# Order of the first loads, the first root and two steps of transposes in the head of an encoder layer

## The chip, the cores and the metric

The kernel runs on one core of a Trainium2 chip. The metric is the device time of one execution in microseconds (us), as the median of several runs; beside it stands one execution that the hardware profiler recorded. TensorE multiplies, VectorE (DVE) and ScalarE (ACT) work on tiles, GpSimd (POOL) and SyncE (SP) mostly start transfers. A transfer that SP starts goes through SP's queue, one that ScalarE starts through ScalarE's own.

## What is computed

One layer on x of 1024 tokens by 1024 features, all float32: half a SwiGLU step, two groups of attention heads on a common projection, and another half SwiGLU step, each between two RMS norms. The change touches only the start of the first step:

```python
def rmsnorm(x, g):
    xf = x.astype(jnp.float32)
    y = xf * lax.rsqrt(jnp.mean(xf * xf, axis=-1, keepdims=True) + NORM_EPS)
    return (y * g.astype(jnp.float32)).astype(x.dtype)

def swiglu(x, w_gate, w_up, w_down):
    return (jax.nn.silu(x @ w_gate) * (x @ w_up)) @ w_down

    ...
        h = swiglu(rmsnorm(x, ffn1_pre_g[l]), ffn1_w_gate[l], ffn1_w_up[l], ffn1_w_down[l])
        x = x + 0.5 * rmsnorm(h, ffn1_post_g[l])
```

## The kernel before

**Tiles.** x is cut into eight tiles of 128 tokens by 1024 features; the head of the kernel works on tiles 0 to 3. A tile is normalised (square and sum, root, scale by the row's root and the gain), and then turned by TensorE's transposes (L174), 128 x 128 at a time, four for a half of 512 features, because the products contract over features. Large products are done in Strassen's way: x and the weights are split into blocks A11, A12 and so on, and seven passes replace eight. Each float32 operand is split into a high part, cast to fp32r (whi, and x by L181), and a low part, the difference (wlo, and x by L182). A product is three matmuls: high by high (L471), high by low of x (L472), low of the weights by high (L477).

**The order of the work.** In the head the order of TensorE, VectorE and ScalarE is the order in which the program names the instructions; an engine doesn't pass one that waits. The transfers of one queue are started in order too. The stages of the head are:

- The loads (L1641 to L1645, and L1653 to L1658): tiles 0 and 1 come as halves of 512 features, the first half on SP's queue and the second on ScalarE's; the row of the norm's gain (`ffn1_pre_g`, 1024 numbers) is SP's second transfer, tile 2 is ScalarE's third. SP then loads the first halves of two weight blocks, tile 3, the second halves, and a third block (`w2`).
- The gain (`spread_gain`, L342): TensorE multiplies the row by a column of ones into two banks, so that every partition has it (L349; the trace shows four matmuls for two). ScalarE copies the two halves out, `gains[0]` and `gains[1]` (L350).
- The squares: tile 0 whole and tile 1's first half on ScalarE (L166), tile 1's second half on VectorE (L1671).
- The root (`rstd_by_sqrt`, L331), a generator in two steps: `next(root)` issues two instructions of VectorE (L335, L336) and the square root of ScalarE (L337); the second `next` issues VectorE's reciprocal and a step of Newton's method (L324 to L327).
- The scaling (L1678) by root and gain, in halves: first the first halves of tiles 0 and 1.
- Transposes of those halves, cast and difference (`op0.one`, which calls `transpose_in`), then the products of blocks 0 and 1 with tiles 0 and 1 (256 columns), then the same for tiles 2 and 3, and last block 2 with all four (512 columns, `soon=True`).

While the loop over the last columns runs, `c.steps` holds the transposes of the tiles' second halves; `PairGemm.mm` (L465) takes one step with `self.c.step()` at fixed points among the four contractions k = 0 to 3. Blocks from the fourth on are fetched by L495, each once VectorE has split the block whose buffer it takes (L1692), and are cast at L461. After the head, TensorE goes on through the passes of the SwiGLU step, the projection and the attention.

Of the kernel before, what the change touches and what calls it, by code (L numbers as in the profile page):

```python
# [102 lines left out]
class Weights:  # L103
# [30 lines left out]
    def next(self):  # L134
        return self.ready.popleft()
# [195 lines left out]
def rstd_by_sqrt(c, ss):  # L331

    nc, k = c.nc, ss.shape[1]
    h, y, e = [c.small.tile([P, 4], F32, tag=t, name=t)[:, :k] for t in ("v", "y", "e")]
    nc.vector.tensor_add(h, ss[:, :, 0], ss[:, :, 1])  # L335
    nc.vector.tensor_scalar(h, h, 0.5 / D, 0.5 * EPS, op0=ALU.mult, op1=ALU.add)  # L336
    nc.scalar.activation(e, h, AF.Sqrt, scale=2.0)  # L337
    yield
    yield newton(c, y, e, h)


def spread_gain(c, t, row, one):  # L342

    nc = c.nc
    copies = []
    for h in range(2):
        sl = slice(h * T, h * T + T)
        ps = c.psm.tile([P, T], F32, tag="mm", name="gps")
        nc.tensor.matmul(ps, one, row[:, sl], start=True, stop=True)  # L349
        copies.append(lambda sl=sl, ps=ps: nc.scalar.copy(t[:, sl], ps))  # L350
    return t, *copies
# [85 lines left out]
class PairGemm:  # L437
# [27 lines left out]
    def mm(self, ps, w, i, a, go_on=False, cols=slice(0, T), ks=range(4), soon=False):  # L465
        hi, lo = w
        xhi, xlo = self.op.x[a]
        mm, out = self.c.nc.tensor.matmul, ps[:, cols]
        for k in ks:
            sl = slice(k * P, (k + 1) * P)  # L470
            mm(out, hi[:, i, sl], xhi[:, k, cols], start=not go_on and k == 0, stop=False, skip_group_check=go_on)  # L471
            mm(out, hi[:, i, sl], xlo[:, k, cols], start=False, stop=False, skip_group_check=go_on)  # L472
            if k == 1 or k == 3 and soon:
                self.c.step()
        for k in ks:
            sl = slice(k * P, (k + 1) * P)
            mm(out, lo[:, i, sl], xhi[:, k, cols], start=False, stop=k == 3, skip_group_check=go_on)  # L477
        if 3 in ks and not soon:
            self.c.step()
# [180 lines left out]
class GatePairs:  # L660

    ties, late, deep, soon = (), (), 3, True
# [340 lines left out]
class QKPairs:  # L1003

    ties, late, deep, soon = (DVE,), (ACT,), 2, False
# [399 lines left out]
def layer(tc, a, out):  # L1405
    nc = tc.nc
    c = Ctx(tc)
    with ExitStack() as ctx:
# [26 lines left out]
        x0 = [a["x"][t * P:(t + 1) * P, :] for t in range(8)]  # L1435
# [51 lines left out]
        def gate_pairs(which, op, wg, wu, early):  # L1487
            return PairGemm(c, op, [(wg[f], wu[f]) for f in range(NF)], early, GatePairs(c, which))

        def ffn(which, op, prep, pg, get, turns, sums, more, post, pre, src, dst, begin=None, tables=()):  # L1490
# [7 lines left out]
            if begin:  # L1498
                left_pool(e)
            begun = begin(pg) if begin else ()  # L1500
            plan(pg.early, turns)
            r = sub()
# [119 lines left out]
        with ExitStack() as order:  # L1622
# [9 lines left out]
            half = [slice(0, T), slice(T, D)]  # L1632
            first_junk = [c.xp.tile([P, D], F32, tag="s", name="junk", bufs=2)]
            w2 = c.xp.tile([P, D], F32, tag="x1", name="w2", bufs=2)
            xn = [c.xp.tile([P, D], F32, tag="xn", name="xn", bufs=c.xn) for _ in range(2)]
            gain = c.xp.tile([P, D], F32, tag="pre", name="gain", bufs=1)
            xs = {t: c.xp.tile([P, D], F32, tag="x", name="x", bufs=4) for t in range(4)}
# [3 lines left out]
            for t in range(2):  # L1641
                for h, q in enumerate((nc.sync, nc.scalar)):
                    q.dma_start(xs[t][:, half[h]], x0[t][:, half[h]])
                    if (t, h) == (0, 0):
                        nc.sync.dma_start(xn[0][:1], a["ffn1_pre_g"])  # L1645
            op0.gain, *gains = spread_gain(c, gain, xn[0][:1], xn[1][:1, :P])

            def begin(pg):
                for b in range(2):
                    pg.raw[b] = c.wg.tile([P, 2, T], F32, tag="g", name="graw")  # L1650
                pg.raw[2] = w2.rearrange("p (i x) -> p i x", i=2)
                for b in range(2):
                    nc.sync.dma_start(pg.raw[b][:, 0], pg.srcs[b][0][:, half[0]])  # L1653
                nc.scalar.dma_start(xs[2], x0[2])
                nc.sync.dma_start(xs[3], x0[3])
                for b in range(2):
                    nc.sync.dma_start(pg.raw[b][:, 1], pg.srcs[b][0][:, half[1]])
# [6 lines left out]
                def square(t, h=None, to=None):  # L1664

                    x = xs[t] if h is None else xs[t][:, half[h]]
                    acc = ss[t // 2][:, t % 2, h or 0:(h or 0) + 1]
                    if to is None:
                        sumsq(c, x, acc, junk()[:, :x.shape[1]])
                    else:  # L1670
                        nc.vector.tensor_tensor_reduce(out=to, in0=x, in1=x, scale=1.0, scalar=0.0,  # L1671
                                                       op0=ALU.mult, op1=ALU.add, accum_out=acc)
# [10 lines left out]
                def parts(b):  # L1683

                    raw = pg.raw.pop(b)
                    w = pg.w[b] = [c.wr.tile(list(raw.shape), F32R, tag="g" + p, name="w" + p) for p in ("hi", "lo")]

                    def hi(i):
                        nc.scalar.copy(w[0][:, i], raw[:, i])

                    def lo(i):
                        nc.vector.tensor_sub(w[1][:, i], raw[:, i], w[0][:, i].bitcast(F32))  # L1692
                        if i and b < 2:
                            pg.fetch_left(b + 3)
                    return hi, lo
# [3 lines left out]
                square(0)  # L1699
                square(1, 0)  # L1700
                square(1, 1, xn[1][:, half[1]])
                gains[0]()
                root = rstd_by_sqrt(c, ss[0])
                next(root)
                (hi0, lo0), (hi1, lo1), (hi2, lo2) = [parts(b) for b in range(3)]
                hi0(0)
                gains[1]()
# [39 lines left out]
                while keeps:  # L1747
# [8 lines left out]
                                    {0: [F(4, 5), L(6, 7)], 2: [F(6, 7)], 3: [U(4)], 5: [U(5)], 6: [U(6)], 7: [U(7)]},  # L1756
                                    down_sums(a["wd1"], ts1), value_sums(a["wv"], tsv),
                                    a["ffn1_post_g"], a["mix_pre_g"], x0, x1, begin,
                                    bias_steps(c, *[a[k] for k in ("na_rel_bias", "t5_rel_bias", "onehot", "lncount", "cmask")]))

# [17 lines left out]
            pg = PairGemm(c, op, [(a["wqk"][p], a["wqk"][8 + p]) for p in QK_ORDER], 8, QKPairs(c))  # L1778
# [163 lines left out]
        with ordered():  # L1942
# [18 lines left out]
            pg = gate_pairs(3, op, a["wg2"], a["wu2"], 11)  # L1961
# [94 lines left out]
```

## Time and profile before

| What | Value |
|---|---|
| Median of 3 runs | 1828.11 us (1826.81 to 1828.82) |
| The profiled execution's own time | 1829.11 us |
| Its span, first to last instruction | 1827.3 us |
| Mean granted TensorE clock of the core | 0.999 |
| First square on ScalarE starts | 4.26 us |
| First product that needs high and low parts starts | 14.57 us |

A row of the timeline reads: start, duration (us from the span's start), engine, line, operation, what it writes and reads, shapes, and in brackets how long the engine sat idle before and what ended that. "SPq" and "ACTq" are a queue's issues, which take the issuing engine's time; the data land later. PEld is TensorE's loading of weights. A row of the table of stretches reads: from and to, length, busy time and number of instructions of TensorE, its weight loads, VectorE, ScalarE and GpSimd, granted clock, DMA share, GB/s. A row of the waits: who waited for whom, us in total, times, longest. A row of the DMA view: queue, packets, MB, share of the 16 DMA engines in that stretch.

### The profile page before, as it was taken

What the parts mean: (1) busy time and instruction counts of PE and PEld (TensorE: products, weight loads), DVE (VectorE), ACT (ScalarE), POOL (GpSimd) and SP (SyncE); (2) the same over time, 40 slices, a digit from 0 to 9 for tenths busy, and PEclk for the clock granted to TensorE, in tenths of its full rate; (3) what the DMA queues carried; (4) which work ended last, traced back from release to release, by engine and by line L of the source; (5) the groups of instructions that cost most, each with busy time, mean ns of one, the idle gap of its engine ahead of it and who ended that gap; (6) DMA issues with size and microseconds to landing.
All of it is one profiled execution on the core that took longest, in us unless ns stands there. A gap on an engine that the chain in (4) does not pass through costs nothing. (4 is left out here: it accounts for less than half of the span.)

```text
span 1827.3 us, 25167 instructions
## 1 busy us (share of the span) xinstructions
PE 1808.0 (99%) x8876; PEld 1524.0 (83%) x8876; DVE 1309.0 (72%) x2225; ACT 831.5 (46%) x1495; POOL 350.2 (19%) x583
## 2 busy tenths in 40 slices
PE   8999999999999999999999999999999999999998
PEld 6888888888888888888999998888888888888886
DVE  5888876776466878477676856788887777654557
ACT  6622233334443656134688765564223333354433
POOL 2223321112021123232344100121111111110000
PEclk9999999999999999999999999999999999999999
DMA  7756566557888857868687523594655566596564
GB/s 274 255 185 219 165 231 218 208 208 253 308 304 308 285 204 263 266 226 297 196 264 245 190 99 115 184 314 166 196 175 199 198 222 225 182 350 198 191 229 145
DMA packets 172769, 409.28 MB, mean 224 GB/s; under 512 B 20401, under 2 KB 42321, under 8 KB 170594
## 3 DMA queue, kind: packets, MB, share of 16 engines
q1 hardware_dynamic: 124450, 246.07, 40.9%
q0 software_dynamic: 47184, 159.51, 24.0%
q10 hardware_dynamic: 1008, 2.10, 0.3%
q8 instruction: 70, 1.15, 0.2%
q14 instruction: 57, 0.47, 0.1%
HBM read 280.09 MB, written 132.56 MB: 226 GB/s over the span
## 5 line engine op out<-in xcount | busy, mean ns | idle before, releaser
L471 PE MATMUL mmp<-x,whi 128*128 128x512 f32 (+1 forms) x1464 | 571.4, 390 | 0.7 <-ACT x L181 0.7
L472 PE MATMUL mmp<-x,whi 128*128 128x512 f32 (+1 forms) x1464 | 569.2, 389 | 0.7 <-DVE x L182 0.6
L789 PE MATMUL accp<-pw 128*128 128x512 f32 x1800 | 410.9, 390 | 0.0
L789 PEld LDWEIGHTS accp<-pw 128*128 128x128 f32 x1800 | 337.4, 188 | 69.7
L477 PE MATMUL mmp<-x,wlo 128*128 128x512 f32 (+1 forms) x1464 | 390.7, 389 | 0.0
L472 PEld LDWEIGHTS mmp<-x,whi 128*128 128x128 f32 x1464 | 275.9, 188 | 57.5 <-DVE x L182 1.5
L471 PEld LDWEIGHTS mmp<-x,whi 128*128 128x128 f32 x1464 | 275.9, 188 | 56.8 <-ACT x L181 1.3
L477 PEld LDWEIGHTS mmp<-x,wlo 128*128 128x128 f32 x1464 | 274.6, 188 | 56.7 <-DVE wlo L462 0.2
L757 DVE TENSOR_TENSOR pw<-praw,pw 128x1024 fp32r<-128x1024 f32 (+1 forms) x181 | 200.1, 1145 | 129.2 <-ACT pw L756 128.4
L756 ACT CAST pw<-praw 128x1024 fp32r<-128x1024 f32 (+1 forms) x181 | 168.6, 983 | 207.1 <-PE accp L789 163.5
L461 ACT CAST whi<-wraw 128x1024 fp32r<-128x1024 f32 x126 | 132.7, 1053 | 190.4 <-PE mmp L472 164.5
L462 DVE TENSOR_TENSOR wlo<-wraw,whi 128x1024 fp32r<-128x1024 f32 x126 | 153.3, 1218 | 2.5 <-ACT whi L461 2.5
L699 POOL DMA_DIRECT2D g<-sg x44 | 24.0, 545 | 428.7 <-DVE sg L692 243.0
L651 DVE TENSOR_TENSOR c<-mmp,u 128x512 f32<-128x512 f32 x52 | 36.0, 691 | 72.1 <-PE mmp L477 72.1
L461 ACT CAST whi<-traw 128x512 fp32r<-128x512 f32 x52 | 32.3, 621 | 120.7 <-DVE traw L560 92.7
L487 ACT COPY s<-mmp 128x512 f32<-128x512 f32 x49 | 28.8, 588 | 126.2 <-PE mmp L477 120.7
L559 DVE TENSOR_TENSOR wraw<-wraw 128x1024 f32<-128x1024 f32 x52 | 63.7, 1224 | 16.4 <-DMA wraw<-in_wu_dram 15.7
L789 PE MATMUL accp<-pw,x 128*128 128x512 f32 x312 | 71.8, 390 | 0.0
L1091 DVE CUSTOM_DVE_ANT_0 s<-sp,g 128x256 f32<-128x256 f32 (+1 forms) x128 | 48.1, 413 | 30.2 <-PE sp L1188 24.4
L789 PEld LDWEIGHTS accp<-pw,x 128*128 128x128 f32 x312 | 58.3, 188 | 12.3 <-DVE pw L757 0.3
L638 DVE TENSOR_TENSOR c<-mmp,v 128x512 f32<-128x512 f32 x52 | 35.8, 689 | 34.0 <-PE mmp L477 34.0
L1337 PE MATMUL po<-vs,pt 128*128 128x128 f32 x352 | 49.9, 276 | 0.9 <-DVE pt L1103 0.9
(282 smaller groups left out, 2490.8 us busy)
## 6 DMA issues: line engine op xcount, KB each, us to landing
praw<-g SPq DMA_DIRECT2D x70, 512.0 KB
wraw<-in_wg_dram SPq DMA_DIRECT2D x44, 512.0 KB
wraw<-in_wu_dram SPq DMA_DIRECT2D x44, 512.0 KB
tr<-in_wd_dram SPq DMA_DIRECT2D x44, 512.0 KB
g<-sg POOLq DMA_DIRECT2D x88, 256.0 KB, 5.2
ts<-tr POOLq DMA_DIRECT2D x22, 1024.0 KB, 4.7
praw<-ts SPq DMA_DIRECT2D x88, 256.0 KB
praw<-in_wd_dram SPq DMA_DIRECT2D x66, 256.0 KB
```

Source lines behind the costliest of these rows:

```text
L461: nc.scalar.copy(hi, raw)
L462: nc.vector.tensor_sub(lo, raw, hi.bitcast(F32))
L471: mm(out, hi[:, i, sl], xhi[:, k, cols], start=not go_on and k == 0, stop=False, skip_group_check=go_on)
L472: mm(out, hi[:, i, sl], xlo[:, k, cols], start=False, stop=False, skip_group_check=go_on)
L477: mm(out, lo[:, i, sl], xhi[:, k, cols], start=False, stop=k == 3, skip_group_check=go_on)
L559: nc.vector.tensor_sub(r[:, 0:2], r[:, 1:3], r[:, 0:2])
L651: c.behind(lambda: nc.vector.tensor_add(c21, d, u2), *((DVE,) if self.sink.soon and b == self.n - 1 else ()))
L756: nc.scalar.copy(hi, raw[:, :m])
L757: nc.vector.tensor_sub(lo, raw[:, :m], hi.bitcast(F32))
L789: c.nc.tensor.matmul(acc[t], a, b, start=not chained and gi == 0 and j == i == 0, stop=end and j + n >= len(ops) and i == len(two) - 1, sk ...
L1091: c.nc.vector.tensor_tensor_reduce(out=s, in0=ps, in1=bias, scale=-1.0, scalar=3e38, op0=ALU.add, op1=ALU.min, accum_out=neg)
L1337: nc.tensor.matmul(po[0][:, u], pt[0][:, j, :], vs[:, k0 + j, :], start=j == 0, stop=j == n - 1)
```

## The change

Three things are changed, all in the head:

1. Loads. The gain's row is started by ScalarE, after the halves of tiles 0 and 1, and no longer by SP between the two tiles. Tile 2 is started by SP, between the first halves of the two weight blocks, and no longer by ScalarE.
2. The first root's first step comes ahead of the gain's first copy in ScalarE's and VectorE's order.
3. In a product with `soon=True` (the third block alone) the two steps are taken after k = 0 and k = 2, where they were taken after k = 1 and k = 3; the other products keep theirs after k = 1 and at the end.

```diff
--- before.py
+++ after.py
@@ -470,7 +470,7 @@
             sl = slice(k * P, (k + 1) * P)
             mm(out, hi[:, i, sl], xhi[:, k, cols], start=not go_on and k == 0, stop=False, skip_group_check=go_on)
             mm(out, hi[:, i, sl], xlo[:, k, cols], start=False, stop=False, skip_group_check=go_on)
-            if k == 1 or k == 3 and soon:
+            if k in ((0, 2) if soon else (1,)):
                 self.c.step()
         for k in ks:
             sl = slice(k * P, (k + 1) * P)
@@ -1641,17 +1641,16 @@
             for t in range(2):
                 for h, q in enumerate((nc.sync, nc.scalar)):
                     q.dma_start(xs[t][:, half[h]], x0[t][:, half[h]])
-                    if (t, h) == (0, 0):
-                        nc.sync.dma_start(xn[0][:1], a["ffn1_pre_g"])
+            nc.scalar.dma_start(xn[0][:1], a["ffn1_pre_g"])
             op0.gain, *gains = spread_gain(c, gain, xn[0][:1], xn[1][:1, :P])
 
             def begin(pg):
                 for b in range(2):
                     pg.raw[b] = c.wg.tile([P, 2, T], F32, tag="g", name="graw")
                 pg.raw[2] = w2.rearrange("p (i x) -> p i x", i=2)
-                for b in range(2):
-                    nc.sync.dma_start(pg.raw[b][:, 0], pg.srcs[b][0][:, half[0]])
-                nc.scalar.dma_start(xs[2], x0[2])
+                nc.sync.dma_start(pg.raw[0][:, 0], pg.srcs[0][0][:, half[0]])
+                nc.sync.dma_start(xs[2], x0[2])
+                nc.sync.dma_start(pg.raw[1][:, 0], pg.srcs[1][0][:, half[0]])
                 nc.sync.dma_start(xs[3], x0[3])
                 for b in range(2):
                     nc.sync.dma_start(pg.raw[b][:, 1], pg.srcs[b][0][:, half[1]])
@@ -1699,9 +1698,9 @@
                 square(0)
                 square(1, 0)
                 square(1, 1, xn[1][:, half[1]])
-                gains[0]()
                 root = rstd_by_sqrt(c, ss[0])
                 next(root)
+                gains[0]()
                 (hi0, lo0), (hi1, lo1), (hi2, lo2) = [parts(b) for b in range(3)]
                 hi0(0)
                 gains[1]()
```

## The prediction

> **What bounds the kernel now.** I read the page's top first, then the table of stretches, then what TensorE waited for, and only then the timeline of the head.
>
> ```profile
> span 1827.3 us, 25167 instructions
> PE 1808.0 (99%) x8876; PEld 1524.0 (83%) x8876; DVE 1309.0 (72%) x2225; ACT 831.5 (46%) x1495; POOL 350.2 (19%) x583
> ```
>
> ```profile
> 0.00:40.00 40.00, 31.12 (x142) 24.80 (x143) 24.65 (x56) 27.74 (x51) 11.93 (x29) 1.00 0.70 256
> 40.00:100.00 60.00, 60.00 (x281) 49.69 (x280) 49.07 (x77) 32.80 (x54) 9.81 (x19) 1.00 0.73 250
> ```
>
> ```profile
> PE gps L349 <- DMA xn<-in_ffn_pre_g_dram: 4.2, 1, 4.2
> PE trp L174 <- DVE xn L1678: 3.3, 1, 3.3
> ...
> PE mmp L472 <- DVE x L182: 0.6, 2, 0.3
> ```
>
> TensorE is busy 99% of the span. Of its 19.3 us of idle time, 8.9 us (40.00 less 31.12) lie in the first 40 us, and from 40 to 100 us it has none. The longest waits are of the head too: for norm's row (4.2), for the first normalised tiles (3.3), for low parts of them (0.6). So what the head gains or loses should reach the end of the kernel one for one, if nothing behind it is as late. The whole change lies in this head; the most it could win is a few us of 1828.
>
> The head, in order of time (start, duration, engine, line, operation):
>
> ```profile
> 1.21 0.32 SPq L1645 DMA_DIRECT2D xn<-in_ffn_pre_g_dram  x1
> 1.57 0.36 SPq L1643 DMA_DIRECT2D x<-in_x_dram  x1
> 1.67 0.46 ACTq L1654 DMA_DIRECT2D x<-in_x_dram  x1
> 4.20 3.75 PE L349 MATMUL gps<-xn 1*128 1x512 f32 x4 [4.20 <-DMA xn<-in_ffn_pre_g_dram]
> 5.26 0.69 DVE L1671 CUSTOM_DVE_ANT_0 xn<-x 128x512 f32<-128x512 f32 x1 [5.26 <-DMA x<-in_x_dram]
> 8.08 0.63 ACT L166 ACTIVATE junk<-x 128x512 f32<-128x512 f32 x1 [2.68 <-DMA x<-in_x_dram]
> 8.84 0.16 DVE L335 TENSOR_TENSOR v<-ss 128x2 f32<-128x2 f32 x1 [2.88 <-ACT junk L166]
> 9.24 0.20 ACT L337 ACTIVATE e<-v 128x2 f32<-128x2 f32 x1
> 9.85 0.58 ACT L350 COPY gain<-gps 128x512 f32<-128x512 f32 x1
> 10.33 1.06 ACT L166 ACTIVATE junk<-x 128x1024 f32<-128x1024 f32 x1
> 10.34 1.41 DVE L1678 SCALAR_TENSOR_TENSOR xn<-x,y,gain 128x512 f32<-128x512 f32 x2
> 11.23 1.94 PE L174 MATMUL trp<-ident,xn 128*128 128x128 f32 x8 [3.29 <-DVE xn L1678]
> 11.29 0.19 ACT L166 ACTIVATION_READ_ACCUMULATOR junk<-x 128x1 f32 x1
> 12.36 0.59 ACT L181 CAST x<-trp 128x512 fp32r<-128x512 f32 x1 [0.88 <-PE trp L174]
> 12.97 0.69 DVE L182 TENSOR_TENSOR x<-trp,x 128x512 fp32r<-128x512 f32 x1 [0.62 <-ACT x L181]
> 13.83 0.69 DVE L182 TENSOR_TENSOR x<-trp,x 128x512 fp32r<-128x512 f32 x1 [0.16 <-ACT x L181]
> 14.57 0.58 PE L472 MATMUL mmp<-x,whi 128*128 128x256 f32 x1
> ```
>
> The chain is read backwards. L472 at 14.57 is the first product that needs the low parts of tiles 0 and 1 (L182, ending 14.52); they wait for the casts, these for the transposes, these for the scaled tiles (L1678 at 10.34), and these for the reciprocal root. That began at 8.84 because ScalarE's square of tile 1's first half waited until 8.08, 2.68 us, for that half, while tile 1's other half had been squared at 5.26. So the first half of tile 1 is what bounds the head. It is SP's third transfer. The shares of the two queues (q1 is SP's, q10 ScalarE's), first from 4 to 5 us, then from 5 to 6, say why:
>
> ```profile
> DMA packets 188, 0.35 MB, mean 352 GB/s; under 512 B 19, under 2 KB 19, under 8 KB 188
> ...
> q1 hardware_dynamic: 96, 0.19, 51.8%
> q10 hardware_dynamic: 92, 0.16, 48.0%
> ```
>
> ```profile
> q10 hardware_dynamic: 67, 0.27, 78.9%
> q1 hardware_dynamic: 48, 0.07, 19.6%
> ```
>
> After 5 us, tile 2 on ScalarE's queue takes four fifths while the rest of tile 1 waits on SP's.
>
> **Part 1: the order of the loads.** Norm's row leaves SP (L1645, 0.32 us) and goes third on ScalarE's queue, in the place at 1.67 that tile 2 had; so ScalarE's issues take no longer, and its table load and first square follow as before. SP issues tile 1's first half some 0.4 us earlier (1.57 less 1.21) and tile 2 (another 0.4 or so) between the first two weight halves, long before these are used. Ahead of tile 2 stand only tiles 0 and 1 and one weight half.
>
> ```profile
> 0.00:4.00 4.00, 0.00 (x0) 0.00 (x0) 0.00 (x0) 1.49 (x2) 0.92 (x9) 1.00 0.46 160
> ```
>
> By 4 us 0.64 MB are moved (160 GB/s), and tiles 0 and 1 are 1.05 MB; at 352 GB/s the rest is in by 5.2 us. Tile 0's 0.52 MB were in at about 3.7 by the same sum and were first used at 4.2, 0.5 later. That makes 5.7 for tile 1; the square at 5.26 says it can be a little sooner. I take 5.6 for tile 1 (bounds 5.26 and 8.08, the two rows of this tile), and 5.6 for norm's row as well, which now stands behind tile 1's half: before, it stood behind tile 0's half and was used with it, at 4.20. The first weight half is in by 5.9 + 0.5, tile 2 by 7.4 + 0.5, tile 3 (behind one more weight half) by 9.7 + 0.5: each before its use below.
>
> Two chains now compete for the first cast:
> - Through tile 1: from square to scaling it is 10.34 - 8.08 = 2.26 us, so 7.9; but the gain's first copy ends near 8.1 (part 2) and holds it until then. From scaling to cast it is 12.36 - 10.34 = 2.02, so 10.1.
> - Through norm's row: TensorE spreads it with four matmuls, 3.75 us, so from 5.6 to 9.35, where it was done at 7.95. ScalarE runs in order: the copy of the gain's second half waits for that, and behind it stand the square of tile 2 and the casts. Copy at 9.4, square 0.48 later (10.33 - 9.85) at 9.88, its sum read 1.15 later (11.29 + 0.19 - 10.33) at 11.03, cast at 11.05.
>
> The second is later: the wait for tile 1 goes, and **norm's row is late next**. The transposes (eight in 1.94) start behind the four matmuls at 9.4 and end at 11.35, beside tile 2's square, so the second cast needn't wait: it follows 0.5 after the first (as 10.33 follows 9.85), at 11.55. L182 for tile 0 starts 0.61 after the first cast (12.97 - 12.36), at 11.66; the one for tile 1 behind it at 12.33, to 13.02. L472 is at 13.07 in place of 14.57: **1.50 us gained**. The squares and root of tiles 2 and 3 hang behind the same casts on ScalarE and VectorE and move with them.
>
> **Part 2: root ahead of the row's copy.** The root (0.20) is issued before the gain's first copy. Before, the copy ran while VectorE made the root's input, and cost nothing (root at 9.24, 0.40 after 8.84). Now the first two of the four matmuls end near 5.6 + 1.9 = 7.5 and the copy near 8.1, while the root's input is ready at 5.6 + 0.76 + 0.40 = 6.8: in the old order the root would start at 8.1, the scaling 1.10 later (10.34 - 9.24) and the cast 2.02 after that, at 11.2, against 11.05 by the row. So the swap is worth 0.2 us; it is cover for part 1, and I count nothing for it by itself.
>
> **Part 3: the transposes of the third block**, after its products k=0 and k=2 in place of k=1 and k=3 (two matmuls earlier each).
>
> ```profile
> 27.68 0.60 PE L174 MATMUL trp<-ident,x 128*128 128x128 f32 x4
> 28.32 0.59 ACT L181 CAST x<-trp 128x512 fp32r<-128x512 f32 x1 [0.66 <-PE trp L174]
> 28.94 0.69 DVE L182 TENSOR_TENSOR x<-trp,x 128x512 fp32r<-128x512 f32 x1 [0.34 <-ACT x L181]
> 29.69 0.50 PE L472 MATMUL mmp<-x,whi 128*128 128x512 f32 x1 [0.22 <-DVE x L182]
> ```
>
> L472 at 29.69 waits for the second L182. A 512 wide matmul takes 0.21 us of TensorE here (60.00 us for 281, in the table of stretches), so two earlier is 0.43 for the transposes and the second cast, which waited 0.66 for them. The second L182 gains less: VectorE was idle only 0.34 before it. So L182 starts 0.34 sooner, and L472 with it: **0.34 gained**. Nothing is added on any engine, the same instructions move. Bounds: nothing, if the cast is held by ScalarE's other copies in that stretch; 0.43.
>
> Who is late next is the fourth block's weights:
>
> ```profile
> 33.01 1.05 ACT L461 CAST whi<-graw 128x1024 fp32r<-128x1024 f32 x1
> 34.81 0.19 PEld L471 LDWEIGHTS mmp<-x,whi 128*128 128x128 f32 x1
> ```
>
> They are cast by 34.06 and loaded at 34.81. Their fetch is released by VectorE's split of the head and moves with part 1; part 3's 0.34 is covered by the slack of 0.75. If the fetch didn't move at all, the sum below would shrink by 1.84 - 0.75 = 1.09.
>
> **The sum**: 1.50 + 0.34 = 1.84 us. From the profiled execution (1829.11, span 1827.3) it gives 1827.27; that run stood 1.00 over the median, so the median of the runs goes from 1828.11 to **1826.3**. 0.2%, about what a measurement of this kernel can tell from no change, is 3.7 us, twice the sum.
>
> **Rivals.**
>
> 1. *The late half was an accident of this execution* (0.25). One slow DMA engine may have held that half until 8.08 in the profiled execution alone. Then the head before was usually not bound by tile 1, its cast came about where norm's row now puts it (11.05, or up to 1.0 sooner, since the four matmuls ended at 7.95), and part 1 is worth 0 to -1.0. With part 3's 0.34 the time is 1827.8 to 1828.8, in the middle 1828.3. For it: the profiled execution was 1.00 over the median. Against: q1's share falls at once when tile 2 comes, which is no accident.
> [...]
>
> 2. *Slower: norm's row takes the wait over in full* (0.1). If it is its row that comes late, at 8.08, as tile 1's half did, the four matmuls end at 11.83, the cast is at 13.5 and L472 at 15.6, 1.0 later than before; less 0.34, **1828.8**. The point from which it decides is a first use of the row at 5.6 + 1.84 = 7.4. For it: the row is now behind two halves; against: nothing follows it on its queue.
>
> 3. *TensorE's clock rises earlier* (0.15).
>
> ```profile
> L471 PE MATMUL mmp<-x,whi 128*128 128x256 f32 x7 | 3.2, 456 | 0.7 <-ACT x L181 0.7
> ```
>
> ```profile
> L471 PE MATMUL mmp<-x,whi 128*128 128x256 f32 x10 | 3.0, 325 | 0.0
> ```
>
> The first row is from 13.8 to 20 us, the second from 20.3 to 25.3: the same matmul takes 456 ns, then 325, though the table of stretches has 1.00 as the granted clock for both. If the faster stage began some 3 us sooner, it would take in the transposes of tiles 2 and 3: eight cost 1.94 at 11.23, four 0.60 at 27.68, so 0.7 is saved: **1825.6**. If it began no sooner than now, the 1.5 us won are spent on more slow work, at that ratio (1.20 to 1.94) some 0.6: 1826.9.
> [...]
>
> **How the numbers follow.** The forecast has 0.5, its own range is 1825.8 to 1827.2 (row used at 5.26 or 6.0, part 3 worth 0 or 0.43, the clock not sooner). The rivals have 0.25, 0.1 and 0.15. The range takes in rival 3 with half a us of the runs' scatter (1826.81 to 1828.82) and most of rival 1: 1824.7 to 1828.4. Faster by over 0.2% means under 1824.45: only rival 3 with luck, 0.06. Slower by over 0.2% needs 1831.8, which no case gives: 0.01. Within it: 0.93.
>
> **What would show it.** Right: the square of tile 1 near 5.6 without the 2.7 us wait; the four matmuls L349 near 5.6 to 9.35; the gain's second copy just behind; the first cast near 11.05 with no wait for the transposes; L472 near 13.1; no idle time ahead of the one at 29; the end 1.8 earlier. Wrong: L349 after 7; the weights' cast at 33 not moved and TensorE waiting for it; or a copy that still waits on a DMA in the first 10 us.

## The result, and the profile after

| | Before | After |
|---|---|---|
| Median of 15 runs each, side by side | 1827.94 us (1825.41 to 1830.22) | 1831.00 us (1828.08 to 1833.95) |
| Profiled execution, its own time and span | 1829.11, 1827.3 | 1829.46, 1827.7 |

The change makes the kernel slower: the ratio is 1.0016, with a 95% interval of 1.0009 to 1.0024. That is 1.6 to 4.4 us, where 1.84 us less were forecast. The profiled execution of the changed kernel stood 1.5 us under its own median, that of the kernel before 1.2 us over its own; so the two traces, laid side by side, show less of the loss than there is. Two of the six runs of e8 below (93.47 and 93.49 us) were slow ones, over 1.5% above the fastest of their kernel; without them its median is 92.60 us in place of 92.83.

The top of the page of after, and the first two rows of its table of stretches (the columns as before):

```profile
span 1827.7 us, 25167 instructions
PE 1807.9 (99%) x8876; PEld 1522.7 (83%) x8876; DVE 1310.1 (72%) x2225; ACT 831.8 (46%) x1495; POOL 351.8 (19%) x583
```

```profile
0.00:40.00 40.00, 30.32 (x142) 23.13 (x143) 25.50 (x56) 27.98 (x51) 11.91 (x29) 1.00 0.77 284
40.00:100.00 60.00, 60.00 (x282) 49.70 (x281) 47.99 (x76) 33.00 (x54) 9.72 (x18) 1.00 0.67 232
```

The same number of instructions, nearly the same busy time, and from 40 to 100 us still no idle time of TensorE. In these 100 us the traces differ in the first 40 alone, where TensorE is idle for 9.7 us instead of 8.9. The head itself, in the timeline of after:

```profile
1.67 0.54 ACTq L1644 DMA_DIRECT2D xn<-in_ffn_pre_g_dram  x1
5.45 0.63 ACT L166 ACTIVATE junk<-x 128x512 f32<-128x512 f32 x1
5.49 3.75 PE L349 MATMUL gps<-xn 1*128 1x512 f32 x4 [5.49 <-DMA xn<-in_ffn_pre_g_dram]
6.95 0.20 ACT L337 ACTIVATE e<-v 128x2 f32<-128x2 f32 x1 [0.78 <-DVE v L336]
9.28 0.58 ACT L350 COPY gain<-gps 128x512 f32<-128x512 f32 x1 [0.60 <-PE gps L349]
10.81 1.06 ACT L181 CAST x<-trp 128x512 fp32r<-128x512 f32 x2
12.76 0.58 PE L472 MATMUL mmp<-x,whi 128*128 128x256 f32 x1 [0.26 <-DVE x L182]
```

Up to here nearly everything is as forecast, and the row is used well ahead of the 7.4 from which rival 2 decides: no wait of 2.7 us ahead of the square, the row used at 5.49 (5.6 was taken), the first cast at 10.81 (11.05), L472 at 12.76 (13.07). TensorE's waits of after, by sum, show what came instead (four rows of that view):

```profile
PE gps L349 <- DMA xn<-in_ffn_pre_g_dram: 5.5, 1, 5.5
PE mmp L477 <- DVE wlo L462: 1.7, 1, 1.7
PE mmp L471 <- ACT whi L461: 1.0, 1, 1.0
PE mmp L471 <- ACT x L181: 0.7, 1, 0.7
```

The second and third rows have no counterpart before. Both are the fourth block's weights: its low part from VectorE (L462) and its high part from ScalarE (L461). This is the timeline of after there:

```profile
30.12 1.28 ACT L678 ACT_TABLE_LOAD   x1
31.41 0.63 ACT L678 ACTIVATE place<-place 128x512 f32<-128x512 f32 x1
31.95 1.03 ACT L461 CAST whi<-graw 128x1024 fp32r<-128x1024 f32 x1
33.03 0.50 PE L471 MATMUL mmp<-x,whi 128*128 128x512 f32 x1 [1.04 <-ACT whi L461]
33.61 0.69 DVE L676 TENSOR_TENSOR place<-mmp,place 128x512 f32<-128x512 f32 x1 [1.25 <-DMA s1d<-place]
34.40 1.28 DVE L229 SCALAR_TENSOR_TENSOR xn<-x,y,gain 128x1024 f32<-128x1024 f32 x1
35.61 1.22 DVE L462 TENSOR_TENSOR wlo<-graw,whi 128x1024 fp32r<-128x1024 f32 x1
36.88 1.20 PE L477 MATMUL mmp<-x,wlo 128*128 128x512 f32 x4 [1.74 <-DVE wlo L462]
```

And of before, the same work (the cast at 33.01 was shown above the prediction's sum):

```profile
34.09 1.28 ACT L678 ACT_TABLE_LOAD   x1
34.24 1.23 DVE L462 TENSOR_TENSOR wlo<-graw,whi 128x1024 fp32r<-128x1024 f32 x1
35.65 0.69 DVE L676 TENSOR_TENSOR place<-mmp,place 128x512 f32<-128x512 f32 x1
37.23 1.28 DVE L229 SCALAR_TENSOR_TENSOR xn<-x,y,gain 128x1024 f32<-128x1024 f32 x1
```

Read the lines in each list from top to bottom: **the order on two engines is another one**. Before, ScalarE casts the weights (L461, 33.01) and then loads the table of the Silu (L678); after, the table load and the first Silu, 1.28 + 0.63 us, stand ahead of the cast. Before, VectorE makes the low part (L462) and then the second addition L676; after, L462 stands behind that addition and behind a scaling (L229, 1.28 us). The addition overwrites `place` while a store out of it has not ended, so it waits 1.25 us for the store, and L462 waits behind it though the cast that it needs ended at 32.98. Nothing in the diff says so: past the first loops of the head a planner, which schedules the program when it is built, orders VectorE and ScalarE, and with two steps of transposes moved by two matmuls it chose another order. What it weighs is not shown here. The account of the kernel before, that the head's order on these engines is the order in which the program names the instructions, holds for TensorE and for the loads, but not here.

The same instruction of TensorE in each trace, as its start in before and its distance from that in the others (us; worked out from the starts in the traces, experiments e1 to e15 are described below):

| Start in before | 4.20 | 13.85 | 24.26 | 29.69 | 32.31 | 35.03 | 37.75 | 93.25 |
|---|---|---|---|---|---|---|---|---|
| after | +1.29 | -1.92 | -2.82 | -3.20 | -3.20 | -2.00 | +0.16 | +0.17 |
| e1, steps alone | +0.16 | -2.17 | -2.39 | -2.78 | -2.79 | -1.58 | +0.14 | +0.17 |
| e2, steps, old order | +0.03 | -0.66 | -1.76 | -2.14 | -2.15 | -1.54 | -1.37 | -1.37 |
| e3, loads and root | +1.31 | -1.91 | -1.90 | -1.90 | -1.92 | -1.92 | -1.92 | -1.92 |
| e4, all, old order | +1.29 | -1.92 | -1.82 | -2.22 | -2.24 | -2.09 | -1.93 | -1.87 |
| e12, row on a third queue | +1.71 | -1.51 | -2.34 | -2.72 | -2.72 | -2.17 | -2.04 | -2.04 |
| e15, row in its old place | +0.14 | -1.64 | -1.65 | -1.64 | -1.63 | -1.63 | -1.63 | -1.63 |

After had won 3.20 us by 29.69 and lost 3.36 between 32.31 and 37.75; 2.8 of these are the two waits above. Two things in the table needed experiments. Why are e1 and e2, which have the old loads, ahead of before at 13.85 as well? And what are the parts worth one by one?

### The profile page after: what moved, and what is told of

It is laid out like the page before. It is cut to its first block, busy times and chain, and to the rows that moved or that the text cites. A ratio compares the mean times of both kernels' runs of the same rounds, so it can differ in the third digit from the quotient of the medians.

```text
span 1827.7 us, 25167 instructions
## 1 busy us (share of the span) xinstructions
PE 1807.9 (99%) x8876; PEld 1522.7 (83%) x8876; DVE 1310.1 (72%) x2225; ACT 831.8 (46%) x1495; POOL 351.8 (19%) x583
## 3 DMA queue, kind: packets, MB, share of 16 engines
q10 hardware_dynamic: 866, 1.58, 0.2%
## 4 chain that ended last, share of the span: by engine, by line
PE 89%; DVE 4%; issue 3%; ACT 2%; DMA 1%; POOL 1%; ACTq 0%; DVEq 0%; POOLq 0%
PE accp L789 22%; PE mmp L477 18%; PE mmp L472 18%; PE mmp L471 18%; PE po L1221 3%; PE ptp L1101 2%; PE po L1337 2%; PE sp L1188 1%; PE sp L1321 1%; PE accp L363 1%; PE accp L362 1%; PE accp L364 1%; PE trp L174 1%; ACT junk L166 1%; DVE pw L757 1%
## 5 line engine op out<-in xcount | busy, mean ns | idle before, releaser
L472 PE MATMUL mmp<-x,whi 128*128 128x512 f32 (+1 forms) x1464 | 569.7, 389 | 0.7 <-DVE x L182 0.7
L477 PE MATMUL mmp<-x,wlo 128*128 128x512 f32 (+1 forms) x1464 | 390.7, 389 | 1.7 <-DVE wlo L462 1.7
L477 PEld LDWEIGHTS mmp<-x,wlo 128*128 128x128 f32 x1464 | 274.5, 188 | 58.7 <-DVE wlo L462 2.4
L472 PEld LDWEIGHTS mmp<-x,whi 128*128 128x128 f32 x1464 | 276.0, 189 | 56.9 <-DVE x L182 1.4
L461 ACT CAST whi<-wraw 128x1024 fp32r<-128x1024 f32 x126 | 132.7, 1053 | 184.9 <-PE mmp L472 159.4
L462 DVE TENSOR_TENSOR wlo<-wraw,whi 128x1024 fp32r<-128x1024 f32 x126 | 153.1, 1216 | 2.7 <-ACT whi L461 2.7
L461 ACT CAST whi<-traw 128x512 fp32r<-128x512 f32 x52 | 32.3, 620 | 123.9 <-DVE traw L560 96.6
L1337 PE MATMUL po<-vs,pt 128*128 128x128 f32 x352 | 50.0, 276 | 0.0
```

The source lines that it names most:

```text
L461: nc.scalar.copy(hi, raw)
L462: nc.vector.tensor_sub(lo, raw, hi.bitcast(F32))
L1337: nc.tensor.matmul(po[0][:, u], pt[0][:, j, :], vs[:, k0 + j, :], start=j == 0, stop=j == n - 1)
```

## The experiments

Those on the whole kernel were timed in five rounds beside the kernel before. The runs of one full kernel scatter by 3 to 7 us, so some compare **cut** kernels, which end soon after the changed part: the first step's first eleven blocks' left halves are computed, one piece is written out, and all that follows (passes, projection, attention, second step) is left out.

```diff
             pg.ahead(begun, ready)
+            if which == 1: return (e.close(), r.close(), w.close(), *[None] * 3)[-4:]
...
             nc.gpsimd.dma_start(d, sg)
+            if b == 10: nc.gpsimd.dma_start(c.o[:, :T], sg)
```

**e1, the moved steps alone** (part 3; loads and root as before).

```diff
-            if k == 1 or k == 3 and soon:
+            if k in ((0, 2) if soon else (1,)):
```

> Only the two steps of the third block are moved (k = 0 and 2); loads and root as before. The instruction order of VectorE and ScalarE differs from before in one place: the fourth block's split (L461, L462) stands behind the Silu's table load and behind the second addition L676. Theory A (the moved split is the cost): slower than before by 2 to 4 us, with TensorE waiting over 1 us for L462 between 33 and 42 us. Theory B (a faster head squeezes the transfers): the head is as before, so faster by 0.2 to 0.4 us or the same, no new wait for L462.

Measured: 1831.2 us (1828.89 to 1832.73), ratio 1.0016 (1.0007 to 1.0025). The one line makes the whole loss. Two rows of TensorE's waits in e1:

```profile
PE mmp L477 <- DVE wlo L462: 1.3, 1, 1.3
PE mmp L471 <- ACT whi L461: 1.0, 1, 1.0
```

**e2, the moved steps with the old order.** The same, and the fourth block's cast and split are held where they were: the first Silu has to come behind the cast, the second Newton step behind the split. These are edges of the issue order; no engine gains a wait on another.

```diff
+def split_first(c):
+    cast, split = [next(i for i in reversed(c.nc.cur_bb.bb.instructions) if i.engine == e) for e in (ACT, DVE)]
+    for late, first in ((c.silu[0].ins, cast), (c.marks[1].ins, split)):
+        c.tc.add_manual_dep(late, first.name, mybir.DependencyInfo(mybir.DependencyClass.NoSync, mybir.DependencyReason.DATA), reason="split_first")
...
-                self.c.behind(lambda: self.split_left(b + 1), *(self.sink.late if b else ()))
+                self.c.behind(lambda: self.split_left(b + 1), *(self.sink.late if b else ())); begun and b == 2 and split_first(c)
```

> As the run with the moved steps alone, but the split L461, L462 is held at its old place in both engines' orders; every engine's order but TensorE's is then that of before. Theory A: the loss is gone; faster than before by 0.2 to 0.5 us. Theory B: same as the run with the moved steps alone, within 0.5 us.

Measured: 1827.6 us, ratio 1.0000 (0.9991 to 1.0009). With the order held, the loss is gone: the medians of e1 and e2 differ by 3.6 us, and nothing differs between the two programs but the order (their intervals, 1.0007 to 1.0025 and 0.9991 to 1.0009, overlap by 0.0002). The expected 0.2 to 0.5 us under before did not come, but that little is less than these runs can tell. Two rows of TensorE's waits in e2 show more:

```profile
PE trp L174 <- DVE xn L1678: 2.6, 1, 2.6
PE mmp L471 <- ACT whi L461: 0.4, 1, 0.4
```

The first row is 3.3 in before. The second has no counterpart there: the cast of the fourth block's weights is what TensorE now waits for.

**e3, loads and root alone** (parts 1 and 2; steps as before, and the planner's order on ScalarE and VectorE in that stretch stays as before).

> Loads and root as changed, steps as before; the split keeps its old place in the order by itself. Theory A: the head's gain reaches the end, faster by 1.0 to 2.5 us. Theory B: the head is 1.5 to 2.5 us sooner, but the fourth block's weights are late and TensorE waits 2 us or more for L461 or L462; no faster than before, or slower.

Measured: 1827.44 us, ratio 1.0000 (0.9991 to 1.0009). Its trace stays 1.9 us ahead of the profiled execution of before all through the head (table), with no wait for the fourth block, yet its median is that of before: neither the expected gain of 1.0 to 2.5 us came nor the expected wait of 2 us.

**e4, the whole change with the old order** (the edit of e2 on the changed kernel).

> The whole change, with the split L461, L462 held at its old place in both engines' orders; all else is instruction for instruction the changed kernel. Theory A: faster than before by 1.5 to 2.8 us, so 4 us or more below the changed kernel; TensorE waits under 0.5 us for the fourth block. Theory B: within 1 us of the changed kernel, with the wait still there under L461 in place of L462.

Measured: 1828.38 us, ratio 1.0007 (0.9998 to 1.0016), against 1.0016 with the new order. TensorE's waits have none for the fourth block any more, as expected, but the 1.5 to 2.8 us under before did not come. Its profiled execution took 1830.11, with a wait of 2.5 us in the attention (L1337), where the trace of before has 0.9 and that of after none; what sets this wait isn't shown.

**e5 to e8, cut kernels**: before, after, loads and root alone, the whole change with the old order. They ran side by side.

> The kernel before, left off after the first eleven blocks' left halves (the products of L471, L472, L477 up to some 70 us); the Strassen passes, the projection, the attention and the second SwiGLU step are left out, and only one piece of the output is written. It is the zero for the three runs beside it; some 75 to 100 us, with a scatter well below that of the whole kernel if the scatter comes from the later stages.

> The changed kernel, left off at the same place. Theory A (the loss of 3 us arises where the split moved, and is larger in executions that aren't profiled): 2 to 4 us above the cut kernel before. Theory C (it arises later, in the passes or the attention): 0.8 us below, as the profiled executions stand to each other at 60 us.

> Loads and root changed, steps as before, left off at the same place. If the head's gain holds until here and is lost or drowned later: 1.5 to 2.1 us below the cut kernel before. If it is given back at once in executions that aren't profiled (theory B): within 0.5 us of it.

> The whole change with the split at its old place, left off at the same place. Theory A: 1.4 to 2.3 us below the cut kernel before, so 4 us or more below the cut changed kernel. Theory B: no lower than the cut kernel before.

Measured: 92.49 (92.15 to 92.62), 94.85 (94.54 to 95.57), 93.08 (92.22 to 93.36) and 92.83 us (92.01 to 93.49). After loses 2.4 us; the order alone is worth 2.0 of them (94.85 less 92.83; with 92.60 it is 2.25). And **the new loads lose**, some 0.6 us (five runs against four, one of the five as low as before), where 1.5 were to be won; e7 and e8 were expected 1.4 to 2.3 us under e5, or level with it. The cut kernel before shows why, in its timeline:

```profile
4.32 3.75 PE L349 MATMUL gps<-xn 1*128 1x512 f32 x4 [4.32 <-DMA xn<-in_ffn_pre_g_dram]
5.72 0.63 ACT L166 ACTIVATE junk<-x 128x512 f32<-128x512 f32 x1
9.99 0.59 ACT L181 CAST x<-trp 128x512 fp32r<-128x512 f32 x1 [0.16 <-PE trp L174]
12.21 0.58 PE L472 MATMUL mmp<-x,whi 128*128 128x256 f32 x1
```

Here the old loads bring tile 1's first half in time: the square starts at 5.72, without a wait, not at 8.08, and L472 at 12.21, not at 14.57. The cut kernel with the new loads, the same lines:

```profile
5.81 0.61 ACT L166 ACTIVATE junk<-x 128x512 f32<-128x512 f32 x1
5.97 3.75 PE L349 MATMUL gps<-xn 1*128 1x512 f32 x4 [5.97 <-DMA xn<-in_ffn_pre_g_dram]
11.29 1.06 ACT L181 CAST x<-trp 128x512 fp32r<-128x512 f32 x2
13.24 0.58 PE L472 MATMUL mmp<-x,whi 128*128 128x256 f32 x1 [0.26 <-DVE x L182]
```

The square is no earlier, norm's row is 1.65 later, and L472 1.03 later. The chain through the row sets the end, as the prediction says, but against a head that wasn't late.

**e9 to e12**, side by side: the cut kernel before again, as a mark; the cut kernel with the moved steps and the old order; the cut kernel with the whole change, the old order, and norm's row started first on GpSimd's queue; and the full kernel of that.

```diff
+            nc.gpsimd.dma_start(xn[0][:1], a["ffn1_pre_g"])
             nc.gpsimd.memset(xn[1][:1, :P], 1.0)
...
-            nc.scalar.dma_start(xn[0][:1], a["ffn1_pre_g"])
```

> The cut kernel before once more, as the mark for the two cut kernels beside it (another chip may stand elsewhere). Both theories: 92.2 to 92.8 us. A further look at the premise of part 1: if the late half was an accident of one execution, the square of tile 1's first half starts at 5.6 to 6.0 with no long wait, as in the first cut run (5.72); if it is regular, at 7.4 to 8.1.

> The cut kernel with the two steps moved and the fourth block's split held at its old place; loads and root as before. If the moved steps cost only through the planner's new order, they are worth here what the stage says: the wait of 0.34 at the third block goes, so 0.3 to 0.5 us under the cut kernel before of this call. If moving the steps itself costs (another wait behind it), the time is 1 us or more above it.

> The cut kernel with the whole change and the old order, but norm's row started first on GpSimd's queue instead of third on ScalarE's. If the new loads lose what they lose because norm's row comes after both tiles (the four matmuls begin near 5.6 to 6.0 instead of 4.3), the row is used near 4.3 again and the time is about 1.0 us under the whole change with the old order, that is at or under the time of the moved steps alone (0.3 to 0.5 us under the cut kernel before). If they lose it elsewhere (tile 2 or the weights), the time stays 0.2 to 0.5 us above the cut kernel before.

> The full kernel of the last: whole change, old order, norm's row first on GpSimd's queue. If the two causes found are all there is, it loses none of the 3 us and gains some 0.4 us in quiet executions and up to 2.5 us in those where the first half of tile 1 comes late: 1825 to 1827.6, a ratio of 0.9985 to 1.0, at the edge of what these runs can tell from before. If the change loses something more, it stands at 1828 or above.

Measured: 91.93 (91.45 to 92.72), 92.54 (91.97 to 93.17), 93.54 (93.14 to 93.68) and, in full, 1827.79 us, ratio 1.0005 (0.9996 to 1.0013).

- e9: the square at 5.72 again, so the quiet head is what the cut kernels with the old loads show, three of three with e10.
- e10 misses its expectation of 0.3 to 0.5 us less; the two ranges of runs overlap. The starts of TensorE's instructions tell more than the medians: against e9 it stands at +0.27 at 25.19, at -0.18 at 29.40 and at +0.45 at 33.62. So the moved steps do win 0.45 at the third block, and 0.63 is lost again at the fourth. Two rows of e10's timeline:

```profile
31.24 1.05 ACT L461 CAST whi<-graw 128x1024 fp32r<-128x1024 f32 x1 [1.25 <-DMA graw<-in_wg_dram]
32.34 0.50 PE L471 MATMUL mmp<-x,whi 128*128 128x512 f32 x1 [0.40 <-ACT whi L461]
```

  The cast waits for the block's fetch, and TensorE for the cast: the wait has moved from the third block to the fourth.
- e11 and e12 miss too, for the edit didn't do what it was made for. From e11's timeline:

```profile
1.32 0.62 POOL L1642 DMA_DIRECT2D xn<-in_ffn_pre_g_dram  x1 [0.38 <-issue]
6.00 3.75 PE L349 MATMUL gps<-xn 1*128 1x512 f32 x4 [6.00 <-DMA xn<-in_ffn_pre_g_dram]
13.27 0.58 PE L472 MATMUL mmp<-x,whi 128*128 128x256 f32 x1 [0.25 <-DVE x L182]
```

  Alone on its queue and issued at 1.32, the row is used no earlier than third on ScalarE's (5.97 in e7). Its place among the other loads isn't told apart from tile 2's or the weights'.

**e13 to e16**, side by side: the cut change where only VectorE's split is put ahead of the second Newton step; the cut kernel with the new loads and root, but norm's row back in its old place on SP's queue; the full kernel of that; and the cut change again, as a mark.

```diff
-    for late, first in ((c.silu[0].ins, cast), (c.marks[1].ins, split)):
+    for late, first in ((c.marks[1].ins, split),):
```

```diff
                     q.dma_start(xs[t][:, half[h]], x0[t][:, half[h]])
-            nc.scalar.dma_start(xn[0][:1], a["ffn1_pre_g"])
+                    if (t, h) == (0, 0): nc.sync.dma_start(xn[0][:1], a["ffn1_pre_g"])
```

> The cut kernel with the whole change, where only VectorE's split of the fourth block is put ahead of the second Newton step and of the gain's scaling L229; it still comes right behind the second addition L676, which waits for the store, and ScalarE's cast stays behind the table load and the first Silu. If the two new orders cost as the waits say (1.4 for the split, 0.9 to 1.0 for the cast), the wait for the split all but goes (L676 near 34.5, split to 36.5, needed at 36.4) and that for the cast stays: about 1.3 us under the cut change of this call. If the cast's place is what costs, and the split only follows it, nothing is gained (within 0.4).

> The cut kernel with loads and root changed but norm's row back in its old place, SP's second transfer; steps as before. If the late row is what the new loads lose, L349 begins near 4.3 and the first product with low parts comes back to 12.2 (13.24 with the row third on ScalarE's queue): 91.9 to 92.5 us, the level of the cut kernel before. If tile 2's or the weights' place loses it, 92.8 to 93.4.

> The full kernel of the last: loads and root changed, row in its old place, steps as before. If the first half of tile 1 comes in time because nothing but weights follows it on either queue, the square of that half starts by 6.0 and the head is at its quiet level in every execution: 0 to 2 us under before, 1825.5 to 1827.5, ratio 0.999 to 1.0. If the half still comes late in some executions, no difference from before.

> The cut kernel with the whole change once more, as the mark of this call: 94.5 to 95.1 us by its first run, with the waits for the fourth block's split (1.4) and cast (0.9 to 1.0) again.

Measured: 93.74 (93.24 to 94.21), 91.67 (91.38 to 92.51), in full 1826.98 us, ratio 0.9999 (0.9991 to 1.0008), and 95.27 (94.80 to 95.72).

- e13 takes 1.5 us off e16 (1.3 was expected). Its timeline:

```profile
34.20 0.69 DVE L676 TENSOR_TENSOR place<-mmp,place 128x512 f32<-128x512 f32 x1 [1.28 <-DMA s1d<-place]
34.60 0.50 PE L471 MATMUL mmp<-x,whi 128*128 128x512 f32 x1 [0.97 <-ACT whi L461]
34.81 1.22 DVE L462 TENSOR_TENSOR wlo<-graw,whi 128x1024 fp32r<-128x1024 f32 x1
36.57 1.09 PE L477 MATMUL mmp<-x,wlo 128*128 128x512 f32 x4
```

  The addition still waits for the store, but only L462 stands behind it, it ends at 36.03, and L477 has no wait at all; the wait for the cast stays at 0.97, where e8's trace has 0.3. So both new orders cost: VectorE's some 1.5 us, ScalarE's some 0.7 by the traces and 0.9 to 1.1 by the medians (e13's 93.74 less e8's 92.83 or 92.60, which were not timed side by side).
- e14 is 1.4 us under e7, from which it differs only by the row's place; the two were not timed side by side, and e16 stands 0.4 over e6, the same kernel in e7's group. Its row is used at 4.93 instead of 5.97, its L472 is at 12.48 instead of 13.24. The late row is what the new loads lose; no loss by tile 2 or the weights is seen (91.67, against 91.93 in e9 and 92.49 in e5).
- e15 makes no difference to before, although the head of its profile is 1.6 us ahead of the profiled one of before. In that profile the half of tile 1 was late again, by 1.12 us, though tile 2 no longer runs beside it on ScalarE's queue:

```profile
4.34 3.74 PE L349 MATMUL gps<-xn 1*128 1x512 f32 x4 [4.34 <-DMA xn<-in_ffn_pre_g_dram]
6.44 0.63 ACT L166 ACTIVATE junk<-x 128x512 f32<-128x512 f32 x1 [1.12 <-DMA x<-in_x_dram]
```

e9, e14 and e16 came out 0.2 to 0.3 us outside the times expected of them. None of the full kernels is faster than before by more than the runs can tell.

## Why the prediction was wrong

**Part 3 is the step that failed worst.** "Nothing is added on any engine, the same instructions move" was true and beside the point. They move on TensorE; on VectorE and ScalarE the planner then chose another order for work some five us later, and that costs 3.6 us of the full kernel (e1 against e2) and 2.0 to 2.25 of the cut one (e6 against e8). The prediction had a rival for a late row, none for an order that changes by itself. Among its signs of being wrong was TensorE waiting for the weights' cast at 33; that came, 1.04 us, but the cast had moved, to 31.95.

**"Who is late next is the fourth block's weights" was right, with too much slack.** The 0.75 came from the profiled execution of before, where the fetch was issued at 25.55 and its last part landed at 32.91, just ahead of the cast at 33.01: the cast went by the fetch there too. In e9 the fetch was issued 3.16 us sooner, at 22.39, but landed only 2.22 sooner, at 30.69. The gain of part 3 was there, 0.38 to 0.45 in each trace that has it (between 24.26 and 29.69 in the table; 0.34 was forecast). In each it was given back, in e2, e4, e10 and e12, with the old order: 0.3 to 0.8 us between 32.31 and 37.75. The timeline of e9:

```profile
30.79 1.05 ACT L461 CAST whi<-graw 128x1024 fp32r<-128x1024 f32 x1 [1.06 <-DMA graw<-in_wg_dram]
31.97 0.42 PE L471 MATMUL mmp<-x,whi 128*128 128x512 f32 x1
```

The cast ends at 31.85 and the fourth block's first product starts at 31.97, so the slack is about 0.1. Part 3 was worth nothing, even undisturbed.

**Part 1 priced a wait that comes and goes.** Rival 1, "the late half was an accident of this execution", had 0.25 and should have had more than the forecast. With the old loads the square of that half started at 8.08 (before), 7.42 (e2), 5.91 (e1), 5.72 (e5 and e9) and 5.65 (e10): late in two traces of six, both of the full kernel. In the trace of before, 15 of the 16 parts whose landing the transfer reports had landed by 5.80 and the last at 8.06, so one part held it. With the new loads it started at 5.39 to 5.91 in ten traces: they do take the lateness away. But norm's row is then used at 5.49 to 6.08 and no longer at 4.20 to 4.46, and L472 follows it by 7.26 or 7.27 us in each of these traces; a quiet old head has L472 at 12.21 (e5), the new ones of the cut kernels have it at 13.21 to 13.35. So the gain is there in a late execution, 1.8 at L472 in after against before, and in a quiet one a loss, as the rival's "0 to -1.0" had it: 1.0 in the cut kernel, 0.4 in the full one (12.76 in after, 12.40 in e1). The medians show neither (e3: 1.0000, within 1.6 us, which leaves no room for 1.9 us won in every execution).
A queue of its own won the row nothing: it came at 5.97 third on ScalarE's queue (e7) and at 6.00 alone on GpSimd's (e11).

"q1's share falls at once when tile 2 comes, which is no accident" was the argument against the rival. It is true of the queues' shares (q1's fell from 51.8% to 19.6%), but one part in 16 was missing, and a mean over all the engines doesn't show it.

**Part 2** was counted as cover. In after the root starts at 6.95, while the gain's first copy has to wait for TensorE's spreading until 7.57; in the old order the root would have stood behind that copy, as the prediction says. What the swap is worth alone wasn't tried. One bound of the forecast does not come out of its own terms: with the row at 6.0 and part 3 at nothing they give 1827.0, not the 1827.2 of its range; it changes nothing here.

**Rival 3 came true beside it.** TensorE's 256 wide matmul falls from 0.41 to 0.28 us at 15.9 in after, as the eight transposes at 16.26 take 1.11 us, where those at 18.37 in before take 1.91. By forms, before from 15.2 to 20.2 us, then after from 15.8 to 20.2:

```profile
L477 PE MATMUL mmp<-x,wlo 128*128 128x256 f32 x6 | 1.7, 415 | 0.0
L174 PE MATMUL trp<-ident,x 128*128 128x128 f32 x8 | 1.9, 420 | 0.0
```

```profile
L477 PE MATMUL mmp<-x,wlo 128*128 128x256 f32 x8 | 1.4, 283 | 0.0
L174 PE MATMUL trp<-ident,x 128*128 128x128 f32 x8 | 1.1, 276 | 0.0
```

That is the 0.9 us between -1.92 and -2.82 in the table. But it isn't the change's: e4, with the same loads, has none of it (-1.92, -1.82), and e5 and e9, the same cut kernel, differ by 0.6 in the same place. Nor is it shown to be the clock: the granted clock reads 1.00 in the rows of both tables of stretches.
The time from the first product to the faster matmuls varies from trace to trace: 4.0 us in after (11.92 to 15.90), 6.4 in before (13.85 to 20.29); what sets it isn't shown. The 3 us by which rival 3 has the faster stage begin sooner are a supposition that no run shows: in after it begins 4.4 us sooner than in before (15.90 against 20.29), and the eight transposes save 0.8 (1.91 less 1.11), where the rival had 0.7.

What stays open: the full kernel loses 3.6 us by the order and the cut one 2.0, with 1.5 (e1 against e2) and 2.0 (after against e4) at 93.25 in the full traces. The rest is within the intervals of the ratios (0.0009, or 1.6 us, either way for each), but whether the later stages add to it was not tried. How often the half of tile 1 comes late, and whether the full kernel has it oftener than the cut one, isn't known either: a profile shows one execution.

## What to carry to other kernels

Where a scheduler orders some of the engines, compare the order of every engine before and after an edit, however small, before any duration is summed: here two moved groups of transposes reordered two other engines, and that was the loss. A wait that one profiled execution shows on a DMA is a premise, not a fact, until other profiles of the same code have it too: the 2.68 us of before were 0.42 in e1 and 0.16 in e9, with the same loads. And slack read in a late execution need not be there in a quiet one: the 0.75 us of before were 0.1 in e9, where the head came sooner, and the next transfer was issued 3.16 us sooner but landed only 2.22 sooner.

## What the runs showed of the hardware

- One of the 16 parts of a 256 KB load landed 2.3 us after the other 15 in before (8.06 against 5.80), with nothing in the program to tell why; with the same loads around it, the half was used at 5.91 in e1.
- A load of 4 KB came no sooner on a queue of its own: issued at 1.32 as the first of GpSimd's, it was used at 6.00 in e11, as against 5.97 from third place on ScalarE's in e7; second on SP's queue, ahead of half of tile 1, it was used at 4.20 to 4.93.
- A write of `place` waited for a store out of it: in the first 40 us of after three such stores took 8.4 us in the median from issue to landing, with the DMA engines at 0.77, and the addition L676 waited 1.25 us for one.

```profile
s1d<-place POOLq DMA_DIRECT2D x3, 256.0 KB, 8.4
```
